# Row tiles in pairs over three PSUM banks, with part of the input loaded by column quarters and transposed in VectorE blocks

## The chip, the cores and the metric

The kernel runs on one core of one Trainium2 chip. The metric is the device time of that core in microseconds (us), smaller being better; where several executions were timed, the median is given. The profile's "span" is a little shorter than that time: in every profiled run here the time was 1.75 to 2.0 us above the span. All experiments ran beside the kernel before on the same chip. Executions of one kernel mostly agree within a few tenths of a per cent; some fall about 1% higher (those of before lie near 166.8 or near 168.4 us, and both count as fast), and a few runs that lay over 1.5% above the fastest of their kernel count as slow and are left out of the ratios.

TensorE (PE in the profile) multiplies matrices into PSUM; VectorE is DVE, ScalarE is ACT, GpSimd is POOL, SyncE is SP. ScalarE computes and, in these kernels, also issues DMAs; those issues stand under ACTq, the ones of SyncE under SPq. Partitions are the 128 rows of a tile in the on-chip memories (the first number of a shape in the profile); an eviction is the copy of a finished PSUM tile into SBUF, the other on-chip memory; a DMA moves its bytes in packets, and a ring is the queue of DMAs of one issuing engine; the granted clock is the share of TensorE's full clock that the profile records.

## The reference

```python
batch, seq, hidden, n_heads = (16, 512, 768, 12)      # head_dim 64, all fp32
y = np.matmul(x, weight)                              # 16x512x768 by 768x768
y = y.reshape(batch, seq, n_heads, head_dim)
y1, y2 = y[..., :32], y[..., 32:]                     # halves of each head
out1 = y1 * cos1 - y2 * sin1                          # cos, sin: 512 x 64,
out2 = y2 * cos2 + y1 * sin2                          # the same for every batch and head
```

The rows make 64 tiles of 128 rows. The matmuls of these kernels contract over partitions, so each tile of x has to stand transposed (the 768 of `hidden` on the partitions, in six chunks of 128) before it can be multiplied by the weight.

## The kernel before

Per tile: a load on SyncE, a cast to fp16 on ScalarE, six transposes on TensorE into PSUM, an eviction on ScalarE, twelve matmuls (six chunks, each cut at column 512, where the next part of the code's PSUM tile `[P, 2, 512]` begins; such a part of 512 fp32 is called a bank here), two multiplies on VectorE, an add on GpSimd, a store issued by ScalarE three tiles later.

```python
SB = 4; NMB = 64; NKT = 6; NSPLIT = [(0, 512), (512, 256)]
xv = x.rearrange("b (p r) h -> b r p h", r=SB)

def load(i):
    xss[i] = xpool.tile([P, H], FP32, tag="xs", name="xs")
    nc.sync.dma_start(out=xss[i], in_=xv[i // SB, i % SB])    # 128 partitions x 3072 bytes

def transpose(i, eng):
    xc = x16.pop(i)
    pt = pt_pool.tile([P, NKT, P], FP16, tag="pt", name="pt")
    for kt in range(NKT):
        nc.tensor.transpose(pt[:, kt, :], xc[:, ts(kt, P)], ident)
    xTT[i] = tpool.tile([P, NKT, P], FP16, tag="xT", name="xT")
    copy(eng, xTT[i], pt)
# ...
def rope(i, c0, n, ps, add_eng):          # broadcasts and rearrangements cut
    nc.vector.tensor_tensor(out=tv, in0=ps, in1=cos_sb, op=MULT)
    nc.vector.tensor_tensor(out=qv, in0=ps_halves_swapped, in1=tee_sb, op=MULT)
    add_eng.tensor_tensor(out=ov[:, ds(c0, n)], in0=tv, in1=qv, op=ADD)
# ...
for i in range(FIRST, NMB):
    # load(i + 5); transpose(i + 1, nc.scalar); cast(i + 2, nc.scalar)
    if i < NMB - 1:
        for kt in range(NKT):
            mm(i, kt)
        rope_whole(i)                     # add on GpSimd
        store(i - 3)                      # nc.scalar.dma_start
# ... last tile in two halves of 384 columns
```

## Time and profile before

| | before |
|---|---|
| time, median of 4 runs | 166.66 us (166.42 to 166.84) |
| span of the profiled run (its time was 168.71 us) | 166.9 us |
| TensorE busy, 40 to 160 us | 120.00 of 120.00 us |
| distance from tile to tile in the chain | 2.285 us |
| transposes on TensorE | 384 instructions, 6 per tile |

The one profile of before comes from an execution in its upper group, about 2 us above the median. The period in the middle runs at full clock and is not touched by this, but the start and the end in this profile may be up to 2 us later than usual.

These are lines of the page of the kernel before: span, busy time of each engine, three strips of 40 slices (each digit is the busy share, or the granted clock, in tenths), the chain by engine, groups (busy us, mean ns of one, idle time before it and what ended most of that), and DMA issues (KB each, us from issue to landing).

```profile
span 166.9 us, 3136 instructions
...
PE 153.6 (92%) x1165; PEld 98.5 (59%) x1165; DVE 122.9 (74%) x142; ACT 97.9 (59%) x127; POOL 114.4 (69%) x67
...
PE   7657699999999999999999999999999999999930
...
PEclk9987999999999999999999999999999999999997
DMA  4999999999999999999999999999999984345544
...
PE 88%; DMA 4%; ACT 2%; DVE 2%; issue 1%; SPq 1%; DVEq 0%
...
L130 POOL TENSOR_TENSOR ov<-tv,qv 128x768 f32<-128x768 f32 x63 | 114.2, 1816 | 47.4 <-DVE qv L122 46.2
L103 PE MATMUL psy<-w_sb,xT 128*128 128x512 f16 x756 | 135.1, 329 | 2.5 <-ACT xT L69 1.8
...
L116 DVE TENSOR_TENSOR tv<-psy,cos_sb 128x768 f32<-128x768 f32 (+1 forms) x65 | 61.4, 944 | 31.7 <-PE psy L103 30.5
...
L93 PE MATMUL pt<-ident,xc 128*128 128x128 f16 x384 | 31.9, 219 | 2.9 <-ACT xc L69 2.2
...
xs<-in_x_dram SPq DMA_DIRECT2D x64, 384.0 KB, 5.6
out_dram<-ov ACTq DMA_DIRECT2D x63, 384.0 KB, 4.8
```

One engine without gaps: from the sixth of the 40 slices to the 38th TensorE is at 9, and its matmuls waited 2.5 us in the whole run. The other engines wait for TensorE (VectorE 30.5 us at `tv`). The DMA strip is at 9 as well, which looks like a second limit; the next view shows how to read it.

The windows view of before gives busy us of each engine in a stretch, then the granted clock, the DMA share and GB/s:

```profile
core 0: us, PE busy (x) PEld busy (x) DVE busy (x) ACT busy (x) POOL busy (x), PEclk, DMA share, GB/s
35.00:43.00 8.00, 8.00 (x64) 5.17 (x62) 6.61 (x8) 5.59 (x8) 6.59 (x4) 1.00 1.03 408
40.00:60.00 20.00, 20.00 (x160) 13.20 (x158) 15.85 (x18) 13.49 (x18) 15.45 (x9) 1.00 0.99 350
40.00:160.00 120.00, 120.00 (x941) 78.92 (x938) 95.88 (x106) 78.60 (x103) 95.35 (x53) 1.00 0.88 314
```

The share counts the time of packets on 16 engines; it was 0.99 at 350 GB/s and 1.03 at 408, so a 9 in the strip does not say how much is being moved. A better gauge is the engine time that 1000 bytes take: share x 16 / rate. Before, from 35 to 43 us, it is 1.03 x 16 / 0.408 = 40 ns per 1000 bytes.

The chain of waits of before, in order of time (start, length, what), gives the period:

```profile
23.69 1.95 PE psy L103 x12
25.97 1.95 PE psy L103 x12
```

One tile costs 25.97 - 23.69 = 2.28 us: 1.95 us of matmuls and 0.33 us of transposes. VectorE has 2 x 0.94 us of work in each period, GpSimd 1.82 us.

### The profile page before, as it was taken

The numbers are of one execution on the slowest core, as the hardware profiler recorded it, in microseconds if no ns is written. First come the engines' busy times: TensorE is split into PE (matmuls) and PEld (weight loads), VectorE is DVE, ScalarE is ACT, GpSimd is POOL, SyncE is SP. The second block draws the span as 40 slices with busy tenths as digits, with TensorE's granted clock in tenths as the row PEclk, the third lists the DMA queues.
The fourth block names the chain that finished last, engine by engine and source line by source line (L and its number), as shares of the span: only waits on it lengthen the run. The fifth ranks groups of instructions, "written<-read, shape, count | busy, mean of one in ns | idle before, by whom it ended". The sixth has DMA issues, their size and how long they took to land.

```text
span 166.9 us, 3136 instructions
## 1 busy us (share of the span) xinstructions
PE 153.6 (92%) x1165; PEld 98.5 (59%) x1165; DVE 122.9 (74%) x142; ACT 97.9 (59%) x127; POOL 114.4 (69%) x67
## 2 busy tenths in 40 slices
PE   7657699999999999999999999999999999999930
PEld 2224466666666666666666666666666666666610
DVE  0522598777877688877778877778877778777792
ACT  3053366667766667766667766667666667666400
POOL 0000099777787777887777887777887777877770
PEclk9987999999999999999999999999999999999997
DMA  4999999999999999999999999999999984345544
GB/s 128 405 402 403 403 404 369 301 375 406 340 372 343 328 350 345 350 326 381 335 327 370 347 330 351 337 327 361 368 349 350 300 323 170 146 161 192 213 166 188
DMA packets 19887, 53.19 MB, mean 319 GB/s; under 512 B 2336, under 2 KB 2848, under 8 KB 19872
## 3 DMA queue, kind: packets, MB, share of 16 engines
q1 hardware_dynamic: 10368, 27.92, 49.5%
q10 hardware_dynamic: 9504, 25.07, 37.8%
q8 instruction: 9, 0.15, 0.5%
q14 instruction: 6, 0.05, 0.1%
HBM read 27.82 MB, written 25.17 MB: 317 GB/s over the span
## 4 chain that ended last, share of the span: by engine, by line
PE 88%; DMA 4%; ACT 2%; DVE 2%; issue 1%; SPq 1%; DVEq 0%
PE psy L103 74%; PE pt L93 13%; DMA xs<-in_x_dram 4%; PE psy L216 1%; DVE ov L130 1%; ACT xc L69 1%; ACT xT L69 1%; DVE qv L122 1%; SPq L80 1%; DVE tv L116 0%; SPq L75 0%; DVEq L130 0%; DVEq L116 0%
## 5 line engine op out<-in xcount | busy, mean ns | idle before, releaser
L130 POOL TENSOR_TENSOR ov<-tv,qv 128x768 f32<-128x768 f32 x63 | 114.2, 1816 | 47.4 <-DVE qv L122 46.2
L103 PE MATMUL psy<-w_sb,xT 128*128 128x512 f16 x756 | 135.1, 329 | 2.5 <-ACT xT L69 1.8
L103 PEld LDWEIGHTS <-xT 128*128 128x128 f16 x756 | 71.8, 99 | 44.9 <-ACT xT L69 2.1
L116 DVE TENSOR_TENSOR tv<-psy,cos_sb 128x768 f32<-128x768 f32 (+1 forms) x65 | 61.4, 944 | 31.7 <-PE psy L103 30.5
L69 ACT COPY xT<-pt 128x768 f16<-128x768 f16 x63 | 50.3, 798 | 51.2 <-PE pt L93 51.2
L122 DVE TENSOR_TENSOR qv<-psy,tee_sb 128x768 f32<-128x768 f32 (+1 forms) x65 | 60.7, 934 | 0.0
L69 ACT CAST xc<-xs 128x768 f16<-128x768 f32 x63 | 52.7, 836 | 5.8 <-DMA xs<-in_x_dram 5.8
L93 PE MATMUL pt<-ident,xc 128*128 128x128 f16 x384 | 31.9, 219 | 2.9 <-ACT xc L69 2.2
L93 PEld LDWEIGHTS <-xc 128*128 128x128 f16 x384 | 26.6, 98 | 12.3 <-ACT xc L69 3.0
L83 DVE CAST w_sb<-w_raw 128x768 f16<-128x768 f32 x6 | 3.3, 558 | 4.1 <-DMA w_raw<-in_weight_dram 4.1
L141 PE MATMUL cold_ps<-cold 128*128 128x512 f16 x13 | 4.6, 514 | 1.2 <-DVE cold L146 1.2
L141 PEld LDWEIGHTS <-cold 128*128 128x128 f16 x13 | 1.5, 126 | 3.3 <-issue 1.9
L71 DVE CAST xc<-xs 128x768 f16<-128x768 f32 x1 | 0.6, 560 | 3.7 <-DMA xs<-in_x_dram 3.7
L69 ACT ACT_TABLE_LOAD x1 | 1.3, 1283 | 2.1 <-issue 2.1
L216 PE MATMUL psy<-w_sb,xT 128*128 128x384 f16 x12 | 2.1, 326 | 0.0
L130 DVE TENSOR_TENSOR ov<-tv,qv 128x384 f32<-128x384 f32 x2 | 1.7, 862 | 0.1
L216 PEld LDWEIGHTS <-xT 128*128 128x128 f16 x12 | 1.2, 98 | 0.8
L71 DVE COPY xT<-pt 128x768 f16<-128x768 f16 x1 | 0.6, 556 | 0.6 <-PE pt L93 0.6
L146 DVE MEMSET cold<- 128x256 uint32 x1 | 0.3, 272 | 0.9 <-PEq L244 0.9
L244 POOL MEMSET const-float32-0.0<- 128x1 f32 x1 | 0.1, 98 | 0.2 <-issue 0.2
L185 DVE TENSOR_SCALAR tee_sb<-tee_sb 128x128 f32<-128x128 f32 x1 | 0.2, 220 | 0.0
L244 POOL MEMSET const-bfloat16-1.0<- 128x1 bf16 x1 | 0.1, 101 | 0.0
(2 smaller groups left out, 0.2 us busy)
## 6 DMA issues: line engine op xcount, KB each, us to landing
xs<-in_x_dram SPq DMA_DIRECT2D x64, 384.0 KB, 5.6
out_dram<-ov ACTq DMA_DIRECT2D x63, 384.0 KB, 4.8
w_raw<-in_weight_dram SPq DMA_DIRECT2D x6, 384.0 KB, 5.9
out_dram<-ov SPq DMA_DIRECT2D x2, 192.0 KB, 2.2
cos_sb<-in_cos_dram ACTq DMA_DIRECT2D x1, 128.0 KB, 5.2
tee_sb<-in_sin_dram ACTq DMA_DIRECT2D x1, 128.0 KB, 6.2
ident<-identity ACTq DMA_DIRECT2D x1, 32.0 KB, 3.6
```

Source lines behind the costliest of these rows:

```text
L69: eng.copy(out=o, in_=i_)
L71: eng.tensor_copy(out=o, in_=i_)
L80: nc.sync.dma_start(out=w_raw[:, kt], in_=wv[:, kt])
L83: nc.vector.tensor_copy(out=w_sb[:, kt], in_=w_raw[:, kt])
L93: nc.tensor.transpose(pt[:, kt, :], xc[:, ts(kt, P)], ident)
L103: nc.tensor.matmul(psys[i][:, ds(noff, nsz)], xTT[i][:, kt, :], w_sb[:, kt, ds(noff % H, nsz)], start=(kt == 0), stop=(kt == NKT - 1),)
L116: nc.vector.tensor_tensor(out=tv.rearrange("p (h d) -> p h d", d=D), in0=ps.rearrange("p (h d) -> p h d", d=D), in1=cos_sb[:, sb, :].unsqu ...
L122: nc.vector.tensor_tensor(out=qv.rearrange("p (h t d) -> p h t d", t=2, d=HD), in0=ps.rearrange("p (h t d) -> p h t d", t=2, d=HD)[:, :, : ...
L130: add_eng.tensor_tensor(out=ov[:, ds(c0, n)], in0=tv, in1=qv, op=ADD)
L141: nc.tensor.matmul(cold_ps, cold[:, 0:P], cold, start=True, stop=True)
L146: nc.vector.memset(cold, 0.0)
L216: nc.tensor.matmul(psys[i][:, n, 0:sz], xTT[i][:, kt, :], w_sb[:, kt, ds(c0, sz)], start=(kt == 0), stop=(kt == NKT - 1),)
```

## The change

The intent is to take work off TensorE, which is the bound.

- Tiles go in pairs. A pair is the same 128 sequence positions of two batches, 2g and 2g + 1. Its 1536 columns lie without a gap in one PSUM tile of three banks, so one VectorE instruction of 3072 results replaces four multiplies, and one GpSimd add replaces two.
- For the odd batches from batch 5 on (groups g = 2 to 7; 24 of the 64 tiles, called block tiles), TensorE no longer transposes. The VectorE transposition used instead turns each 32x32 block within itself. So the load itself moves the blocks into place: each quarter of the columns goes to its own 32 partitions, four DMAs of 32 partitions per batch, two on SyncE's ring and two on ScalarE's. The batches of three groups are asked for in pairs 2, 4 and 6, those of the other three in pairs 10, 14 and 18.
- The order of the contraction is permuted (weight rows and fp16 pairs) so that a transposition of 4-byte words serves two fp16 values at once.
- The last two pairs and the start are arranged anew.

The core of the diff, cut:

```diff
-    def load(i):
-        xss[i] = xpool.tile([P, H], FP32, tag="xs", name="xs")
-        nc.sync.dma_start(out=xss[i], in_=xv[i // SB, i % SB])
+    def by_blocks(n, s):                         # n: pair, s: which batch of it
+        return n // SB > 1 and s == 1
+    def load_blocks(g):
+        xb = bpool.tile([P, SB * NQ, H // NQ], FP32, tag="xb", name="xb")
+        src = x[2 * g + 1].rearrange("(c a) (q k) -> q a c k", a=R, q=NQ)   # R = 32, NQ = 4
+        for q in (0, 2, 1, 3):
+            eng = nc.sync if q < 2 else nc.scalar
+            eng.dma_start(out=xb[ts(q, R)], in_=src[q])      # 32 partitions, 512 packets of 768 bytes
# ...
+    def transpose_blocks(n, s):
+        xT = tpool.tile([P, NT, P, 2], FP16, tag="xT", name="xT")
+        nc.vector.transpose(
+            out=xT.bitcast(FP32).rearrange("p t m e -> p (t m e)"),
+            in_=x16.pop((n, s)).bitcast(FP32),
+        )
# ...
-    py_pool: bufs=3 of [P, 2, 512]
+    py_pool: bufs=2 of [P, 3, 512]
# ...
+    for n in range(2, NP - 1):                   # NP = 32 pairs
+        load_plain(n + DEPTH - 4)
+        if n in (2, 4, 6):
+            load_blocks(n // 2 + 1)
+        elif n % SB == 2:
+            load_blocks(n // SB + 3)
+        if n + 1 < NP and by_blocks(n + 1, 1):
+            transpose_blocks(n + 1, 1)
+        # ... projection of the pair's first tile, transposes and casts of the next pairs
+        if n < NP - 2:
+            for c in CHUNKS:
+                mm(n, 1, *c)
+            rope_add(n)                          # one multiply, one add for the pair
+        else:
+            for c in CHUNKS:
+                mm(n, 1, *c, [0])                # pair 30: columns up to 1024 first
+            rope_add(n, 0, 1024)
+            for c in CHUNKS:
+                mm(n, 1, *c, [1])                # then 1024 to 1535, same PSUM tile
+            rope_add(n, 1024, 2 * H)
+        # ...
+        if n >= 3:
+            store(n - 3, nc.scalar)
# ... last pair (31) in parts, the second tile's projection in two PSUM tiles of the other pool
```

(The two lines on `py_pool` are shortened; the rest is as in the code.)

## The prediction

> **What bounds the kernel now.** TensorE. The windows view has it busy 20.00 of every 20 us from 40 to 160 us; the chain of waits gives it 88% of the span. Period: 2.285 us per 128-row tile (distance of the chain's pieces): 1.95 us of matmuls, 0.33 us of transposes. VectorE is busy about 80% (two 0.95 us multiplies per tile), GpSimd 80% (one 1.816 us add), ScalarE 66%. Outside the steady state: tile 4's matmuls start only at 23.7 us, and 6.8 us follow the last matmul (160.1).
>
> **What the change does.**
> 1. It takes the TensorE transposes from 24 of 64 tiles: 24 × 0.334 = 8.0 us, all on the critical path. A pair with one block tile costs 4.236 us instead of 4.57.
> 2. It merges a pair's four multiplies into one of 3072 results. The traced 384-wide (0.545 us) and 768-wide (0.945 us) multiplies give 1.04 ns per element plus 0.145: about 3.35 us instead of 3.8. [...] Sum 3.85 of 4.236 us: just under TensorE.
> 3. GpSimd adds a pair at once, at most 2 × 1.816 = 3.63 us: off the path, unless the half-swapped operand is slow.
> 4. ScalarE loses 24 evictions of 0.80 us and gains queue work: off the path.
> 5. Block loads use 768-byte packets. From the traced packets (46 ns for 1 KB, 121 ns for 3 KB) one takes about 37 ns, so a block tile costs 1.17 us of the 16 DMA engines instead of 0.97. A pair then needs 0.97 + 1.17 + 1.94 = 4.08 of 4.236 us: 96%, against 85% before. Before's DMA share of 0.99 is not saturation: from 35 to 43 us it moved 415 GB/s, while a period needs 344 (371 after). [...]
> 6. Start: four x tiles come before the weights. The sixth weight should land near 13.5 us, cosine and sine (256-byte runs) near 17; the first multiply then frees pair 0's banks at about 20.7, when pair 2 starts; before, that tile started at 23.7.
> 7. Tail: about 4 us of VectorE behind the last matmul, then a store of some 3 us: 7 us, as now.
>
> **Sum.** Pair 2 at 20.8; six pairs of 4.57 less one tile's transposes = 27.1; 23 pairs of 4.236 = 97.4; last pair 3.9; tail 7.1: 156.3 us. I predict **156.5 us**, 8 times in 10 between 153.5 and 161. Chances: faster by over 2%: 0.90; within 2%: 0.08; slower: 0.02.
>
> **What shows each step.** Right: TensorE busy from 21 to 149 us; period 4.57, then 4.24; 240 transposes instead of 384; multiply near 3.35 us, [...] add under 3.65. Wrong: gaps before projections released by VectorE, or by casts waiting for block loads; an add over 4.2 us, which would make GpSimd the bound.
>
> **What would make it wrong.** Block loads that halve the DMA rate; strided stationary loads that slow transposes and projections; slow strided casts; ScalarE's queue held by issuing 512-row loads; a throttled clock while TensorE waits at the start.

(One number in it is off: the rate from 35 to 43 us, put at 415 GB/s, is 408 in the line shown above.)

(Three passages are cut from it, with the cuts marked: in point 2 a term for the block transpose, with which VectorE's sum came to the 3.85 us that still stand there, and the same term again under "What shows each step"; in point 5 the reason given why the span of 32 partitions should cost nothing further. The sum of 156.3 us holds none of these terms. The 37 ns of point 5 are an estimate from before's packets, which took 46 ns for 1024 bytes and 121 ns for 3072 in the median, 122 and 145 ns in the mean of the two rings. The dangers in the last lines were guesses. What the runs show of them, besides what follows below: a transpose on TensorE took 224 ns in after and 219 in before, a cast on ScalarE 897 to 902 ns and 836, and before's granted clock was 0.50 from 11.1 to 14.4 us.)

## The result, and the profile after

| | before | after |
|---|---|---|
| time, median | 166.66 us | 175.02 us (174.47 to 176.62, 4 runs) |
| ratio to before | | 1.052 (95%: 1.045 to 1.059) |
| span of the profiled run | 166.9 us | 173.6 us |

The kernel became 5% slower; 156.5 us had been predicted. A ratio here is the mean time of one kernel's fast runs over the mean of the other's fast runs of the same rounds, so it is not quite the ratio of the medians quoted. The profiled run took 175.35 us.

The same lines of the page of after:

```profile
span 173.6 us, 2568 instructions
...
PE 153.7 (89%) x1032; PEld 93.7 (54%) x1032; DVE 127.3 (73%) x75; ACT 81.0 (47%) x101; POOL 108.0 (62%) x37
...
PE   7999799994939999999999999889999999965930
...
PEclk9999999997896999999999999999999999996596
DMA  4999999999999999999999999999965444558434
...
PE 57%; DMA 27%; DVE 5%; ACT 3%; issue 2%; SPq 1%; ACTq 1%; DVEq 0%
...
L161 PE MATMUL psy<-w_sb,xT 128*128 128x256 f16 (+1 forms) x756 | 135.4, 335 | 11.5 <-ACT xT L76 7.3
L192 POOL TENSOR_TENSOR ov<-tq 128x1536 f32<-128x1536 f32 (+3 forms) x33 | 107.8, 3293 | 59.2 <-DMA out_dram<-ov 30.4
L181 DVE TENSOR_TENSOR tq<-psy,csn 128x3072 f32<-128x3072 f32 (+3 forms) x33 | 105.9, 3211 | 30.0 <-PE psy L161 29.1
...
L123 PE MATMUL pt<-ident,xc 128*128 128x128 f16 x240 | 20.6, 224 | 0.0
L130 DVE STREAM_TRANSPOSE xT<-xc 128x384 f32<-128x384 f32 x24 | 13.7, 569 | 1.9 <-ACT xc L76 1.9
...
out_dram<-ov ACTq DMA_DIRECT2D x30, 768.0 KB, 8.0
xs<-in_x_dram SPq DMA_DIRECT2D x40, 384.0 KB, 9.9
xb<-in_x_dram SPq DMA_DIRECT2D x12, 384.0 KB, 10.0
xb<-in_x_dram ACTq DMA_DIRECT2D x12, 384.0 KB, 10.7
```

The work left TensorE as intended: 240 transposes instead of 384, 20.6 us instead of 31.9. But TensorE's matmuls now wait 11.5 us, there are holes in its strip in slices 10 and 12 and near the end, its granted clock falls to 0.50 around the end of each hole (from 41.3 to 44.6 us, from 51.5 to 54.8 and from 157.3 to 164.1; 1.00 from 38 to 41.2 and from 44.7 to 51.4), and plain x loads land after 9.9 us where they took 5.6. TensorE's total of busy time did not fall (153.7 against 153.6 us) although there is less to do: twelve matmuls that took 2.11 us elsewhere took 3.60 and 3.19 us where the clock fell, all counted as busy, and after has 22 matmuls of the code's helper `warm` where before had 13 (8.0 us and 4.6 us in the groups view).

The windows view of after, cut where pair 8 starts (56.6 us) and where pair 30 starts (152.0 us), columns as above:

```profile
20.40:56.60 36.20, 30.68 (x211) 19.16 (x211) 20.59 (x7) 18.15 (x24) 24.11 (x7) 0.91 1.07 313
56.60:152.00 95.40, 93.66 (x662) 58.78 (x660) 84.56 (x44) 52.73 (x67) 72.94 (x22) 1.00 0.90 320
152.00:173.60 21.60, 11.18 (x54) 5.71 (x52) 12.13 (x10) 1.29 (x2) 10.74 (x5) 0.78 0.53 203
```

This gives a ledger against the prediction's own sum, in span: pair 2 starts at 20.41 us (predicted 20.8).

| stretch | predicted | measured | difference |
|---|---|---|---|
| start of pair 8 | 47.9 | 56.65 | +8.75 |
| start of pair 30 | 141.1 | 151.97 | +10.9 (2.1 more) |
| from there to the end | 15.2 | 21.6 | +6.4 |
| sum | 156.3 | 173.6 | +17.3 |

(A further 1.75 us is the distance from the span to the time, which the prediction's sum left out.) So the middle of the kernel does what was promised, and the loss sits in the six pairs before pair 8, while three of the six block batches are being loaded, and in the tail. In the first stretch TensorE was idle for 36.20 - 30.68 = 5.5 us; the rest of its loss is slow clock (a mean of 0.91 over 36.20 us).

Who ended the waits is shown by the waits view of after (engine, line, waited for: us in total, times, longest):

```profile
POOL ov L192 <- DMA out_dram<-ov: 30.4, 7, 7.6
...
ACT xT L76 <- DMA xb<-in_x_dram: 12.3, 4, 4.4
...
PE psy L161 <- ACT xT L76: 7.3, 4, 2.8
ACT xT L76 <- DMA out_dram<-ov: 5.9, 1, 5.9
...
PE psy L161 <- DVE tq L181: 4.2, 2, 3.2
```

The second and fourth lines look impossible at first: the eviction `xT` reads PSUM and has nothing to do with a load of `xb` or with a store. The timeline of after between 38 and 54 us explains them (start, us, engine, line, instruction, count, [idle before it and releaser]):

```profile
40.29 0.41 ACTq L211 DMA_DIRECT2D out_dram<-ov  x1
40.75 0.80 ACT L76 COPY xT<-pt 128x768 f16<-128x768 f16 x1 [4.42 <-DMA xb<-in_x_dram]
...
41.60 3.60 PE L161 MATMUL psy<-w_sb,xT 128*128 128x512 f16 x12 [2.76 <-ACT xT L76]
...
46.85 2.83 ACTq L97 DMA_DIRECT2D xb<-in_x_dram  x2
49.72 0.80 ACT L76 COPY xT<-pt 128x768 f16<-128x768 f16 x1 [5.92 <-DMA out_dram<-ov]
...
50.58 3.19 PE L161 MATMUL psy<-w_sb,xT 128*128 128x512 f16 x12 [2.75 <-ACT xT L76]
```

ScalarE started its instructions in the order of the program. The TensorE transposes that the first of these evictions copies had ended by 36.6 us; ScalarE was idle for 4.42 us, until a quarter load had landed, then issued a store (40.29 us), and only then began the eviction (40.75). The second eviction came after the issue of two quarter loads (46.85 to 49.68 us), with 5.92 us of idle time that ended when a store had landed; its transposes had ended by 45.6 us. In this trace a store or a quarter load that ScalarE was to issue thus held ScalarE until an older DMA had landed; the evictions and casts behind it were late, and TensorE waited for them. After each such wait twelve matmuls took 3.60 and 3.19 us; elsewhere in the same view twelve take 2.11. The granted clock was 0.50 from 41.3 to 44.6 and from 51.5 to 54.8 us, and 1.00 between, from 44.7 to 51.4 (0.79 in the mean from 40 to 56.6 us). TensorE's idle times were 2.76 and 2.75 us, up to 41.60 and 50.58 us, with six transposes of 0.50 us in all just before each, so that 3.1 us passed from the end of one projection to the start of the next.

The tail of after in the timeline:

```profile
152.06 3.36 DVE L181 TENSOR_TENSOR tq<-psy,csn 128x3072 f32<-128x3072 f32 x1 [0.39 <-PE psy L161]
...
155.83 2.25 DVE L181 TENSOR_TENSOR tq<-psy,csn 128x2048 f32<-128x2048 f32 x1
...
158.14 6.33 PE L161 MATMUL psy<-w_sb,xT 128*128 128x512 f16 x18 [3.24 <-DVE tq L181]
```

Pair 30 is multiplied in two parts that share one PSUM tile. The matmuls of the second part wait for VectorE's multiply of the first part (the trace names it as what ended the wait, although the columns differ); 3.24 us are lost, and the next 18 matmuls take 6.33 us, with a granted clock of 0.50 from 157.3 to 164.1 us. (An estimate: by their columns, 12 of 512 and 6 of 256, they should take 5/3 of a tile's 1.95 us, 3.25 us; so the low clock costs about 2.9 us. The text for the next run put the usual time at 2.9 us, which is too little.)

### The profile page after: what moved, and what is told of

Read it like the earlier page. It is cut to its first block, busy times and chain, and to the rows that moved or that the text cites. A ratio compares the mean times of both kernels' runs of the same rounds, so it can differ in the third digit from the quotient of the medians.

```text
span 173.6 us, 2568 instructions
## 1 busy us (share of the span) xinstructions
PE 153.7 (89%) x1032; PEld 93.7 (54%) x1032; DVE 127.3 (73%) x75; ACT 81.0 (47%) x101; POOL 108.0 (62%) x37
## 4 chain that ended last, share of the span: by engine, by line
PE 57%; DMA 27%; DVE 5%; ACT 3%; issue 2%; SPq 1%; ACTq 1%; DVEq 0%
PE psy L161 47%; DMA xb<-in_x_dram 15%; DMA xs<-in_x_dram 6%; DMA out_dram<-ov 5%; PE pt L123 5%; DVE tq L181 4%; PE cold_ps L215 4%; ACT xc L76 2%; ACT xT L76 1%; ACTq L211 1%; SPq L83 1%; SPq L97 0%; DVE ov L192 0%; DVEq L353 0%; DVE xT L130 0%
## 5 line engine op out<-in xcount | busy, mean ns | idle before, releaser
L161 PE MATMUL psy<-w_sb,xT 128*128 128x256 f16 (+1 forms) x756 | 135.4, 335 | 11.5 <-ACT xT L76 7.3
L192 POOL TENSOR_TENSOR ov<-tq 128x1536 f32<-128x1536 f32 (+3 forms) x33 | 107.8, 3293 | 59.2 <-DMA out_dram<-ov 30.4
L181 DVE TENSOR_TENSOR tq<-psy,csn 128x3072 f32<-128x3072 f32 (+3 forms) x33 | 105.9, 3211 | 30.0 <-PE psy L161 29.1
L76 ACT COPY xT<-pt 128x768 f16<-128x768 f16 x38 | 30.4, 800 | 67.1 <-PE pt L123 45.5
L76 ACT CAST xc<-xs 128x768 f16<-128x768 f32 x38 | 34.3, 902 | 5.9 <-DMA xs<-in_x_dram 5.9
L76 ACT CAST xc<-xb 128x768 f16<-128x768 f32 x24 | 21.5, 897 | 0.0
L123 PEld LDWEIGHTS <-xc 128*128 128x128 f16 x240 | 17.3, 100 | 6.4 <-issue 0.9
L123 PE MATMUL pt<-ident,xc 128*128 128x128 f16 x240 | 20.6, 224 | 0.0
L130 DVE STREAM_TRANSPOSE xT<-xc 128x384 f32<-128x384 f32 x24 | 13.7, 569 | 1.9 <-ACT xc L76 1.9
L215 PE MATMUL cold_ps<-cold 128*128 128x512 f16 x22 | 8.0, 521 | 1.2 <-DVE cold L220 1.2
```

What stands on the lines that cost most here:

```text
L76: eng.copy(out=o, in_=i_)
L123: nc.tensor.transpose(pt[:, t, e, :], xc[:, t, e, :], ident)
L130: nc.vector.transpose(out=xT.bitcast(FP32).rearrange("p t m e -> p (t m e)"), in_=x16.pop((n, s)).bitcast(FP32),)
L161: nc.tensor.matmul(psys[key][:, ds(pos, hi - lo)], xTT[n, s][:, t, e, :], w_sb[:, t, e, ds(lo, hi - lo)], start=((t, e) == CHUNKS[0] and n ...
L181: nc.vector.tensor_tensor(out=tq.rearrange("p j (h d) -> p j h d", d=D), in0=ps.rearrange("p (h d) -> p h d", d=D) .unsqueeze(1).broadcast ...
L192: eng.tensor_tensor(out=ovs[n][:, ds(c0, w)].rearrange("p (h t d) -> p h t d", t=2, d=HD), in0=tq[:, 0].rearrange("p (h t d) -> p h t d", ...
```

## Experiments

Two theories stood at first. The rate theory: loads into 32 partitions move bytes slowly and slow down all other DMAs, and everything else follows from late DMAs. Its rival, the queue theory: the rate would do, but the issues on ScalarE's queue hold ScalarE, so it is the placing of the issues that costs. Within the rate theory it was open whether the 768-byte packets or the span of 32 partitions is to blame. "T30" below is the start of pair 29's multiply in the trace, which is the start of pair 30 on TensorE within 0.1 us; it was predicted at 141.1 and measured at 151.97 in after. "Wrong" means that the data land elsewhere and the result is wrong, while all instructions, bytes and waits stay.

In the texts below, theory Q is the queue theory and theory R the rate theory. Clauses that named a mechanism which no run here shows are cut from them, with the cuts marked. Where a cut took a theory's name or condition with it, the range behind the cut is, in cols_128 and rows_32, the one for the case that the span of partitions costs the rate, and in same_half the one for the case that it matters which half of the partitions both rings write; the range of same_half_2 is for that case too.

### tail_whole: pair 30 without the cut

```diff
-        if n < NP - 2:
+        if n < NP - 1:
```

> The changed kernel with one thing undone: the next-to-last pair's second projection is issued whole, with one multiply, not cut at column 1024. In the trace of the changed kernel TensorE waits 3.24 us there for a multiply and then runs 18 matmuls at half clock (6.33 us where about 2.9 are usual). If that wait comes from the cut, this kernel saves 4 to 6.5 us: about 169 to 171 us, with no wait of TensorE for VectorE near 155 us. If it is only VectorE running late, the wait moves to the last pair's start and the time stays within 1.5 us of 175. Either way the stalls of the first 56 us stay (about 9 us).

Measured: 173.37 us, ratio 1.040 (1.034 to 1.047), correct result. No wait of TensorE is left in the tail, and it takes 18.2 us from T30 (153.72) where after took 21.6. The tail is 3.4 us shorter, but the median gained only 1.7 us, less than expected: in this trace the middle came 1.7 us later, although the program up to pair 30 is the same. Executions of one kernel differ by as much (172.98 to 175.28 us here); why was not found. That VectorE's own work bounds the tail once the wait is gone is read from the trace. What follows: the cut costs about 3 us of tail in the traces; the larger loss is elsewhere.

### spread: block loads one group per four pairs

```diff
-        if n in (2, 4, 6):
-            load_blocks(n // 2 + 1)
-        elif n % SB == 2:
-            load_blocks(n // SB + 3)
+        if n % SB == 2:
+            load_blocks(n // SB + 2)
```

> The changed kernel, but the first three batches that are loaded by quarters are asked for one by one at pairs 2, 6 and 10, not at pairs 2, 4 and 6. Theory Q (ScalarE's in-order queue is held at DMA issues [...], and the evictions behind them come late) says the holds come from too many transfers in flight early: TensorE's 8.9 us of loss before pair 8 shrinks to under 4 us, time about 169 to 171. Theory R (the 768-byte, 32-partition block loads deliver too slowly, however they are queued) says the loss moves to later pairs: the time stays within 2 us of 175.

Measured: fast runs of 173.38 and 173.46 us, ratio 1.038 (1.033 to 1.043); two further runs, the profiled one among them, were slow (176.4 and 176.7 us). The fast runs are about 1.6 us under after's median, so spreading the loads out takes away little of the loss. In the slow profile T30 is 155.01, and TensorE waits 4.6 us for evictions before 60 us and 4.7 us after it; where the loss lies in the fast runs was not seen.

### rows_128: the same bytes in 128 partitions (wrong)

```diff
-        src = x[2 * g + 1].rearrange("(c a) (q k) -> q a c k", a=R, q=NQ)
+        src = x[2 * g + 1].rearrange("(q p) h -> q p h", q=NQ)
-            eng.dma_start(out=xb[ts(q, R)], in_=src[q])
+            eng.dma_start(out=xb[:, ts(q, NQ)].rearrange("p j k -> p (j k)"), in_=src[q])
```

> WRONG RESULT ON PURPOSE: each block batch is loaded by four DMAs of 128 partitions with 3072-byte rows, on the same two queues, at the same places and of the same bytes; everything else as changed, so VectorE transposes data in the wrong layout. Theory R: with full-speed packets the backlog goes: loads land within 7 us, ScalarE's holds fall from about 21 us to under 6, time about 165 to 168 (the tail's 6.6 us stays). Theory Q: the count of DMAs and the order of the waits are unchanged and so are the front-loaded bytes: holds stay over 12 us and the time over 171.

Measured: 164.30 us, ratio 0.984 (0.980 to 0.987); relative error 0.75, as intended. T30 is 142.04: of the 10.9 us lost before pair 30, 9.9 came back. The queues, places, bytes and number of DMAs are those of after, so the placing of issues alone is not the cause. ScalarE's evictions were held by DMAs for 2.9 us, where after had 12.3 + 5.9; the waits view of rows_128:

```profile
ACT xT L76 <- DMA xs<-in_x_dram: 2.9, 2, 1.6
```

The windows view of rows_128, while the first quarters are being loaded, reads:

```profile
24.00:30.00 6.00, 6.00 (x50) 4.00 (x49) 3.58 (x2) 3.96 (x5) 5.05 (x3) 1.00 1.03 402
```

and the same stretch of after:

```profile
24.00:30.00 6.00, 6.00 (x50) 4.03 (x49) 3.88 (x2) 3.92 (x6) 5.04 (x2) 1.00 1.10 279
```

Both keep the DMA engines fully occupied (1.03 and 1.10), but one moves 402 and the other 279 GB/s. Over the whole stretch from 20.4 to 56.6 us it is 396 and 313. The slow quarters also slow the rest: the packet records of the two kept traces give 196 ns for a packet of a plain load in after from 24 to 30 us, and 125 ns in rows_128.

### all_sp: all loads and the loop's stores on SyncE

```diff
-            eng = nc.sync if q < 2 else nc.scalar
+            eng = nc.sync
-            store(n - 3, nc.scalar)
+            store(n - 3, nc.sync)
```

> All loads by quarters and all stores of the loop are issued from SyncE's queue; ScalarE issues none until the last pair. Results stay right. Theory Q: ScalarE is never held, TensorE has no wait for an eviction after 21 us, time about 165 to 168 (tail's 6.6 us left in). Theory R: [...] casts wait for loads: TensorE's loss stays over 7 us and the time over 172.

Measured: 172.54 us, ratio 1.031 (1.024 to 1.037), correct. T30 is 150.14. ScalarE is not held at an issue before the last pair now, but its casts wait for plain loads instead, and TensorE's transposes for the casts, as the waits view of all_sp shows; and the rate in the same stretch is lower still:

```profile
ACT xc L76 <- DMA xs<-in_x_dram: 24.9, 13, 6.2
...
PE pt L123 <- ACT xc L76: 7.3, 3, 4.1
```

```profile
24.00:30.00 6.00, 6.00 (x50) 4.03 (x49) 4.18 (x2) 3.93 (x6) 5.04 (x2) 1.00 1.11 219
```

Without ScalarE's holds 2.5 us came back, not 11. This run alone would not settle it, because SyncE is now held in its turn, at stores that wait for GpSimd (47.0 us in all in its waits view; GpSimd's adds are 8% of its chain), and the plain loads stand behind them. Together with rows_128, where the issues are placed as in after and the loss is gone, the queue theory falls: the held queue carried the delay to TensorE.

### cols_128: 768-byte packets, but 128 partitions (wrong)

```diff
-        src = x[2 * g + 1].rearrange("(c a) (q k) -> q a c k", a=R, q=NQ)
+        src = x[2 * g + 1].rearrange("(c p) (q k) -> q p c k", p=P, q=NQ)
-            eng.dma_start(out=xb[ts(q, R)], in_=src[q])
+            eng.dma_start(out=xb[:, ts(q, NQ)], in_=src[q])
```

> WRONG RESULT ON PURPOSE: the block batches come in 768-byte packets as in the changed kernel, as many and on the same queues, but each DMA spreads over all 128 partitions (four column quarters, each for all rows) instead of 32. Theory size (the 768-byte packets alone cost the rate: 37 ns for a quarter of the bytes of a 121 ns packet[...]): packet time stays near 47 to 50 ns and the time at 172 to 176. [...] packet time falls to 36 to 39 ns and the time to 164.5 to 167.5.

Measured: 166.30 us, ratio 0.993 (0.985 to 1.002); T30 143.86; the 768-byte packets took 38.6 to 41.3 ns on average (47 to 50 in after). In the stretch from 24 to 30 us of cols_128:

```profile
24.00:30.00 6.00, 6.00 (x50) 4.02 (x49) 3.89 (x2) 3.92 (x6) 5.05 (x2) 1.00 1.08 345
```

### rows_32: 3072-byte packets, but 32 partitions (wrong)

```diff
-        src = x[2 * g + 1].rearrange("(c a) (q k) -> q a c k", a=R, q=NQ)
+        src = x[2 * g + 1].rearrange("(q c a) h -> q a c h", a=R, q=NQ)
-            eng.dma_start(out=xb[ts(q, R)], in_=src[q])
+            eng.dma_start(
+                out=xb[ts(q, R)].rearrange("a (c j) k -> a c (j k)", c=SB), in_=src[q]
+            )
```

> WRONG RESULT ON PURPOSE: the converse: 3072-byte packets, a quarter as many, but each DMA still fills only 32 partitions. [...] these packets grow well over 121 ns on average (150 to 200) and the time stays at 171 to 176. Theory size: they stay at 121 to 135 ns and the time falls to 164 to 167, as when 128 partitions were used with such packets.

Measured: 174.54 us, ratio 1.044 (1.035 to 1.053); T30 154.68. Over the whole run the mean packet of 3072 bytes, plain loads and stores included, took 133 ns on one queue and 146 on the other, below the expected range; but from 24 to 30 us, where nearly all are quarters, the packet records give 191 ns, within it (125 in rows_128). The rate in that stretch of rows_32 fell as it does in after:

```profile
24.00:30.00 6.00, 6.00 (x50) 3.96 (x49) 3.72 (x2) 3.94 (x6) 5.05 (x3) 1.00 1.03 263
```

The last two runs with after and rows_128 make a square that separates the two suspects:

| | 3072-byte packets | 768-byte packets |
|---|---|---|
| 128 partitions | rows_128: 164.30 us, T30 142.0, 402 GB/s, 41 ns per 1000 bytes | cols_128: 166.30 us, T30 143.9, 345 GB/s, 50 ns |
| 32 partitions | rows_32: 174.54 us, T30 154.7, 263 GB/s, 63 ns | after: 175.02 us, T30 152.0, 279 GB/s, 63 ns |

(The ns are share x 16 / rate, worked out from the lines shown. The times are medians, the T30 come from the profiled runs; that of rows_32 took 176.75 us, 2.2 us above its median, so its T30 is late by up to as much.) Going from 128 to 32 partitions costs 8.7 to 10.2 us at the two packet sizes; going from large to small packets costs about 2 us in 128 partitions, where the intervals of the ratios just touch, and nothing that can be read in 32. The rows that rows_32 reads in each DMA are those of rows_128, so which part of memory is read is not the cause either.

### all_pe_tail: no block tiles, tail uncut

```diff
-        return n // SB > 1 and s == 1
+        return False
-        if n < NP - 2:
+        if n < NP - 1:
```

> The pair part alone: no batch by quarters, every tile transposed by TensorE (384 transposes), next-to-last pair whole. If the pair scheme itself is sound, TensorE has no wait after 21 us, pairs follow each other in 4.57 us, pair 30 starts near 20.4 + 28 x 4.57 = 148.4 us, and the time is 165 to 168, about that of the kernel before: the three microseconds won at the start are given back in a longer tail. If the pairs, the larger stores or the held ScalarE queue are a loss of their own, it is over 170.

Measured: 168.76 us (167.78 to 170.2), ratio 1.007 (0.998 to 1.016). T30 is 147.95, the period 4.57 us, and TensorE's only wait is 1.5 us, just before pair 2. So the pairs, the merged multiplies and the new start cost nothing in the steady state, and bring nothing either; the whole gain and the whole loss of the middle hang on the block tiles.

### few_tail: three groups by blocks, tail uncut

```diff
-        return n // SB > 1 and s == 1
+        return n // SB in (3, 5, 7) and s == 1
-        if n in (2, 4, 6):
-            load_blocks(n // 2 + 1)
-        elif n % SB == 2:
-            load_blocks(n // SB + 3)
+        if n % SB == 2:
+            load_blocks(n // SB + 2)
```

(and the uncut tail as above.)

> A version that may win: quarters and VectorE transposes only for the batches of groups 3, 5 and 7 (12 tiles), asked for two groups ahead; next-to-last pair whole. It takes 12 x 0.334 = 4.0 us from TensorE and adds three block batches to the DMA engines, about 7 us of their time instead of 14, spread out. If what counts is that the DMA engines must keep up on average, there are no long waits and the time is about 4 us under the pair part alone: 161 to 164. If each block batch holds ScalarE whenever it comes, stalls of 2 to 3 us per batch eat the gain: 166 to 171.

Measured: 171.49 us, ratio 1.024 (1.016 to 1.032), correct; 7 us and more over the hoped-for range, half a microsecond over the other. TensorE has one long wait, 4.5 us for an eviction near 43 to 48 us, behind quarter loads whose issue held ScalarE for 6.6 us, until a store had landed. One early group of quarter loads, with the DMA engines already full (1.03 at 409 GB/s from 35 to 43 us), is enough to make a stall in this trace.

### same_half and same_half_2: both rings on the same half of the partitions

```diff
-        for q in (0, 2, 1, 3):
-            eng = nc.sync if q < 2 else nc.scalar
+        for q in (0, 1, 2, 3):
+            eng = nc.sync if q % 2 == 0 else nc.scalar
```

In after the two rings load into opposite halves (partitions 0 to 63, and 64 to 127) at any time; here both load into the same half.

> The changed kernel with the quarters re-paired: the two queues now load partitions 0 to 31 and 32 to 63 at one time, then 64 to 95 and 96 to 127, where the changed kernel pairs 0 to 31 with 64 to 95. Same bytes, packets, queues and right results. [...] the stretches in which both queues carry quarters fall from 240 to 340 GB/s to about 210 to 230, and the time is 177 to 184. If only the count of partitions in one DMA matters (32), nothing changes: 173.5 to 176.5.

Measured: 180.97 us, ratio 1.076 (1.069 to 1.084), correct. One run of 883.88 us, which happened to be the profiled one, is an outlier and left out; so the kernel was looked at once more:

> The re-paired quarters once more, unchanged, for a clean trace: one execution of the earlier run lasted 884 us and it was the profiled one. [...] both queues in one half give 210 to 237 GB/s in the stretches that carry only quarters, mean packet time 56 to 60 ns, time 179 to 182.

Measured: 180.42 us (one run, state unknown), correct; in the same stretch of same_half_2:

```profile
24.00:30.00 6.00, 6.00 (x51) 3.99 (x49) 4.12 (x2) 3.92 (x6) 5.03 (x2) 1.00 1.11 224
```

This is 79 ns per 1000 bytes. So opposite halves on two rings do help (279 against 224 GB/s, and 4 to 6 us of time; a sixth of the bytes in that stretch of after are plain loads, here 4%), but they come nowhere near the 402 of 128 partitions.

### all_pe_lag2: as all_pe_tail, stores one pair earlier

```diff
-        if n >= 3:
-            store(n - 3, nc.scalar)
+        store(n - 2, nc.scalar)
```

(on top of all_pe_tail; the store of pair n - 3 after the loop goes as well, here and in the runs that follow.)

> The pair part alone with the next-to-last pair whole, and each pair stored two pairs later instead of three. In the run of the pair part alone three stores of 768 KB and more were still to go out at the last matmul, and 4.45 us passed from the last add to the end, where 2.93 pass in the kernel before. If the late stores make the tail long, the last store lands about 1.5 us sooner: 165.5 to 167.5. If not, the time stays at 167.8 to 170.

Measured: 168.11 us, ratio 1.003 (0.998 to 1.008), correct (the median has one slow run in it). It missed the expected range. Its ratio and that of all_pe_tail overlap, so an effect of the earlier stores is not shown; it would be about 0.4%.

### late_2, late_3 and few_late: fewer and later block tiles

All three have the uncut tail and the earlier stores. late_2:

```diff
-        return n // SB > 1 and s == 1
+        return n // SB in (5, 7) and s == 1
-        if n in (2, 4, 6):
-            load_blocks(n // 2 + 1)
-        elif n % SB == 2:
-            load_blocks(n // SB + 3)
+        if n % SB == 2:
+            load_blocks(n // SB + 2)
```

> As the previous kernel, with quarters and VectorE transposes for the odd batches of groups 5 and 7 only (8 tiles), asked for two groups ahead, when the loads of the start are long done. It takes 8 x 0.334 = 2.7 us from TensorE. If the DMA engines have that much to spare by then, no wait for an eviction longer than 0.5 us and 2 to 2.7 us under the previous kernel: 163 to 165. If a block batch holds ScalarE at any time, 166 to 169.

Measured: 166.05 us (165.45 to 168.98, the highest a slow run), ratio 0.990 (0.985 to 0.995), correct. TensorE's only wait is 1.3 us, just before pair 2. The range was missed, but because all_pe_lag2 itself is slower than had been expected: late_2 is 2.1 us under it in the same rounds, of the 2.7 us that its eight block tiles take from TensorE. So block tiles do pay where their loads do not make TensorE wait. This is the only correct kernel here that is faster than before, by 1%: within the 2% that count as the same, but with an interval that leaves out 1. Against the lower group of before's executions alone (166.72 to 167.01 us) it is half of that.

late_3 adds group 6:

```diff
-        return n // SB > 1 and s == 1
+        return n // SB in (5, 6, 7) and s == 1
```

> As the previous kernel with groups 5, 6 and 7 (12 tiles, 4.0 us of TensorE). With quarters at 210 to 340 GB/s, the three batches cost some 11 us more DMA time than plain loads in some 55 us; in the pair part alone 15 percent of the DMA time is to spare. If that holds: 161.5 to 164. If it is too much, holds of ScalarE come back: 165 to 168.

Measured: a median of 172.51 us, but four of the six runs were slow, the profiled one among them; the two fast ones took 169.86 and 171.83 us, ratio 1.019 (1.010 to 1.029), correct; a miss. In the slow profile TensorE waits 6.1 us for evictions, four times, at most 3.8 us; no fast one was taken, so what the fast runs wait for is not shown. By the fast runs alone, three batches in a row are too many, although two apart are not.

few_late has three groups apart from each other (3, 5 and 7), asked for at pairs 8, 15 and 22:

```diff
-        return n // SB > 1 and s == 1
+        return n // SB in (3, 5, 7) and s == 1
-        if n in (2, 4, 6):
-            load_blocks(n // 2 + 1)
-        elif n % SB == 2:
-            load_blocks(n // SB + 3)
+        if n in (8, 15, 22):
+            load_blocks(3 + 2 * (n // 7 - 1))
```

> Groups 3, 5 and 7 again (12 tiles), asked for at pairs 8, 15 and 22, so that the first no longer meets the loads of the start and no two are in flight together; next-to-last pair whole, stores two pairs later. If separate batches can be absorbed one at a time, there is no stall like the 4.6 us one of the earlier run with these groups, and the time is 163.5 to 166. If three batches are too many wherever they lie, 168 to 173.

Measured: 167.10 us, ratio 0.999 (0.991 to 1.007), correct. Its twelve block tiles should save 12 x 0.33 = 4 us over all_pe_lag2 (168.11 us) and save about 1 (from other rounds, and the intervals overlap); TensorE waits 1.7 us just before pair 2 and then 2.4 us in all, at most 1.9 at once. A miss again, though without a long stall.

### rows_128_tail: what the change would be worth

This is rows_128 with the uncut tail and the earlier stores: everything of the change except loads into 32 partitions and the cut.

> WRONG RESULT ON PURPOSE: full-row, 128-partition loads in place of the quarters, the next-to-last pair whole and stores two pairs later. It asks what is left of the prediction's error once the rate of the block loads and the cut of the next-to-last pair are both taken away. In the full-row run pair 30 began at 142.0 us (predicted 140.7); from there 18.0 us to the end were measured without the cut. So the span should be about 160 us and the time (about 1.8 us over the span in the runs so far) 161 to 162.5. If it is over 163.5, something else is lost that is not named yet; under 160, the tail was worth more than thought.

Measured: 163.27 us, ratio 0.977 (0.972 to 0.982; the interval reaches under 2%), span 161.3. T30 is 143.18 (two early gaps of 0.9 us, for evictions), and 18.1 us follow. Against the prediction's sum, 156.3 + 2.1 (T30 later than 141.1) + 2.9 (tail longer than 15.2) = 161.3 of span, and 1.8 more of time. Such a sum always closes; what the run shows is that 12.3 of the 17.3 us of span are gone with the two faults (and with the earlier stores). It missed its range by 0.8 us.

## Why the prediction was wrong

Point by point, in its own numbering:

1. **TensorE's saving: right.** 240 transposes; once loads have settled, the pieces of the chain stand 4.235 us apart (4.236 predicted), and from 56.6 to 152 us TensorE is idle for 1.74 us of 95.40.
2. **VectorE: right.** The whole-pair multiply took 3.358 us (about 3.35) and the block transpose of 128x384 words of 4 bytes 0.569 us, 3.93 us together of a period of 4.235 (the sum was 3.85).
3. **GpSimd: right.** The whole-pair add took 3.469 us, under 3.63.
4. **"ScalarE loses 24 evictions of 0.80 us and gains queue work: off the path": wrong.** Its busy time fell, from 97.9 to 81.0 us, but 12.3 + 5.9 us of its idle time before evictions ended only when a DMA had landed, and TensorE waited behind these evictions. The busy time did not show this. rows_128 and all_sp show together that this was the way the delay took, not its source.
5. **Block loads of 1.17 us a tile, with a packet of about 37 ns: this is the step that failed.** The packets took 47 to 50 ns, and with 48.5 ns the prediction's own sum gives 512 / 16 x 48.5 = 1.55 us for a block tile, 0.97 + 1.55 + 1.94 = 4.46 us per pair, more than the period of 4.236. The sum holds only while one batch of quarters comes per four pairs; after asks for half of its batches in pairs 2 to 6, and that is where the engines fell behind: full (1.07) at 313 GB/s from 20.4 to 56.6 us, where rows_128 moved 396. The square of four runs shows that the span of 32 partitions is the cause: the loss before pair 30 is 0.9 us in rows_128 and 2.8 in cols_128, against 10.9 in after and 13.6 in rows_32 (in its slower profiled run). The prediction named the danger among its last lines ("block loads that halve the DMA rate") and gave it almost no weight. Its reason for expecting no such loss was not shown by any trace. In all_sp (219 GB/s) and same_half_2 (224) the stretch from 24 to 30 us carries almost only quarters. In after the mix of quarter loads with other traffic moved 27% more with two rings on opposite halves (279 against 219), a part of it because more plain loads were in the mix, but far less than the 402 of rows_128. No run shows where in the chip the rate is lost; what is shown is the span of partitions and which half.
6. **Start: right.** Pair 2 started at 20.41 us (20.8 predicted). The 3 us gained on before may be less, since before's 23.7 us are of a slower execution.
7. **"Tail ... 7 us, as now": wrong.** From the start of pair 30 the sum had 15.2 us and the trace shows 21.6. The cut inside one PSUM tile made a new dependency: 3.24 us of waiting and, by the estimate above, about 2.9 us of low clock (0.50 granted) on the 18 matmuls behind it. Uncut, 18.2 us are left; the last 3 us over the prediction are VectorE's backlog and the landing of the last stores (2.4 to 3.4 us in after), which were argued from the trace and not tested singly.

The direction was wrong, not only a size: 8 us of TensorE work were really removed from the bound, and 17.3 us of span came in elsewhere against the sum, 8.75 of them before pair 8. With both faults taken out, rows_128_tail is 2.3% faster than before, so even a repaired change would not have reached 156.5 us.

What stays open: why late_3 is some 5 us slower than late_2 in fast runs, and why few_late gains only about 1 us of 4. In late_3 the DMA engines are already full (1.02 at 398 GB/s from 40 to 60 us of its slow profile) when the quarters come, but which transfer delays which was not taken apart in either. Nor is it known why the last three batches of after cost so little: from 56.6 to 100.6 us, while they were loaded, the DMA share was 1.03 and TensorE was idle for only 0.4 us. Nor does any run show by what rule an issue waits for an older DMA; the traces show only which landing ended the wait.

## What to carry to other kernels

By these runs, judge a DMA by how many SBUF partitions it spans, before bytes and packet size: here transfers into 32 partitions kept the DMA engines as full and moved 263 to 279 GB/s where 128 partitions moved 345 to 402 (219 to 224 when only one half was written at a time), and plain loads landed later meanwhile, so the full-looking DMA share must be read together with GB/s. In these kernels the engine that computes and also issues DMAs turned a late DMA into a stall of its computing, up to 6.6 us, and the three TensorE stalls of 2.75 to 3.24 us in after cost another 1.1 to 2.9 us each at a granted clock of 0.50. Cutting a projection finer within one PSUM tile added a dependency that cost about 3 us of tail: look for such a one in the built program before counting on the overlap.
